# A new order of the seven products in a bidirectional encoder's Strassen-like projections

## The chip, the cores and the metric

The kernel runs on one core of a Trainium2 chip. The metric is device time in microseconds (us) of one execution; less is better. The core has engines that work side by side, each through a queue of its own: TensorE (PE in the profile, its weight loads PEld), VectorE (DVE), ScalarE (ACT), GpSimd (POOL) and SyncE (SP, which here only issues transfers). Matrix products land in PSUM, which the kernel divides into eight banks of 128 x 512 numbers.

## What is computed

One layer of an encoder over 1024 positions of width 1024, all in float32. A normalised input goes through one wide projection whose columns feed a convolution branch, a gated linear recurrence with eight heads in both directions, and two gates. The branches are merged, projected (w_out) and added to the input. A feed-forward part follows:

```python
h = _rmsnorm(x, attn_norm_w[layer])
y = _token_mixers(h, w_in[layer], ...)
x = x + jnp.einsum("bsd,de->bse", y, w_out[layer])
h2 = _rmsnorm(x, ffn_norm_w[layer])
gate, val = jnp.split(h2 @ ffn_w_up, 2, axis=-1)
x = x + (silu(dwconv3(gate)) * val) @ ffn_w_down
return _rmsnorm(x, final_norm_w)
```

The time goes into the matrix products: w_in (1024 x 8192 columns), ffn_w_up (1024 x 5632), and the smaller ones.

## The kernel before

**Numbers in two parts.** To keep float32's accuracy, each operand is split: ACT rounds it to a part "hi" (L121, a CAST in the profile), DVE subtracts that from the source for a part "lo" (L118). A product of a 128 x 128 block of weights with 128 x 512 activations is then three matmuls (`mm3`, lines L143, L144, L145): hi hi, hi lo, lo hi. The helper `split` does both steps; so the lines L121 and L118 stand for all splits, and only the names of the tiles tell them apart. Activations are kept as pages `hx` and `hy`, weights as `wp` (pool mp, 4 buffers) and `wq` (3 buffers).

**Pair jobs.** Two column blocks of 128 of a weight matrix are multiplied together by `pair_job` (L224), with seven products in place of eight, as Strassen and Winograd do it. The depth of 1024 is cut into two halves of four blocks (nk = 4), the positions into two halves of 512. Operands 1 to 7 on the side of the activations are sums and differences of the quarters, made once; operand 1, 2 and 3 are quarters themselves. On the side of the weights `prep` loads the rows of the first block (`wr`), the columns (`sw`) and the last quarter (`w4`), and lets POOL's accumulating transfers (L238) form sums: `sw` plus the second block, then `wr` plus half of `sw`, then one half of `wr` onto the other. Four splits lie between them: of `wr` for products 1 and 2, of `sw` for 7 and 5 (a `wq` pair of pages), of `wr` for 6 and 3, and of `w4` for 4 (the third `wq` page). `sw` and `w4` have one buffer each.

`run` multiplies: 12 matmuls a product, in the order 1, 2, 6, 7, 5, 4, 3 on three PSUM banks, `row` (of 3 banks "mm"), `b2` (of 2 "tr") and `col` (of 2 "sc"). A product may go on accumulating in a bank that has been copied out. ACT copies the banks after 1, 6 and 7 (L266, tiles `su`), and `evac(e, half, x0, x1, op)` takes a result out of the bank, e being the column block and half the half of the positions.

There are 39 pair jobs: 17 in the projection w_in (stage "in pairs", beside the convolution's 120 DVE operations on L645), 22 in the feed-forward part, where e = 0 is the gate and e = 1 the value. There, the gate's evacuation for half 1 starts the three-tap convolution, silu and the products with `rstd2` and the value (L1162 to L1180), ending in stores to `d_g`.

**Order of the work.** TensorE's instructions stand in the order of the program (`manual_schedule`). Those of the other engines are put in order before the run by the framework, which may draw an instruction forward as soon as its tiles and inputs are planned to be ready; each engine then works through its list in order and waits at whatever is not ready. `Stream` and `run_jobs` interleave jobs with other work: `run_jobs(..., 4)` prepares the next job's weights after four pieces (two products) of the current one.

**Memory.** Pools are stacked. `fw` (L1061) is opened after the heads' pool, before the output projection of the heads (`o_jobs`, L1083) and lives until the feed-forward part ends; `p4` above it holds `mg` (the merged branches, read by the w_out jobs), `x2` and `xq` and is released at L1136; `fu` (L1139) then takes p4's place. A tile in fu waits for the p4 tiles on whose memory it lies. After the feed-forward part `fd` takes the place of fw and fu; its first tiles are `xr`, which lie where `rstd2` was.

**Around the feed-forward part.** While w_out's jobs run, the normalised rows come out as `xq`; for each of the four k, operands 1, 2, 6 and 5 are made there (L1126 to L1135) into pages `hx`, and the rows are stored to `d_h2`. After two products of the first feed-forward job and the statistics for `rstd2` (L420 and L412 on TensorE), the "late" operands 7, 4 and 3 are made (L1209 to L1219): loads from `d_h2` through four `ft` pages, arithmetic on DVE, and a split into pages `hy`. Before that, `bm_loads` (L1002) loads and splits the operands of o_jobs through four `tm` pages. After the feed-forward part the down projection loads `d_g` through `ev` pages and splits it into `hx`; its first results are copied to `xr` (L1245).

Of the kernel before, what the change touches and what calls it, by code (L numbers as in the profile page):

```python
# [10 lines left out]
F32 = mybir.dt.float32  # L11
# [4 lines left out]
ALU = mybir.AluOpType  # L16
# [28 lines left out]
def tile_hybrid_encoder(  # L45
# [45 lines left out]
    def nm(s):  # L91
        uid[0] += 1
        return f"{s}_{uid[0]}"
# [3 lines left out]
    def bank(tag):  # L97
        return ps.tile([P, H], F32, tag=tag, name=nm(tag), bufs=BANKS[tag])
# [125 lines left out]
    def pair_job(src0, src1, nk, acts, wpool, pool, evac, su=4):  # L224

        def prep():
            def both(src, alt):
                hi, lo = split(w_page(2 * nk, alt), w_page(2 * nk, alt), src, V)
                return [(hi[:, :nk], lo[:, :nk]), (hi[:, nk:], lo[:, nk:])]

            def add(o, a):
                G.dma_start(o, a, accum_op=ALU.add)  # L238
# [48 lines left out]
    def combos(ops, k, b11, b12, b22, alloc):  # L287

        def sub(o, a, b):
            V.tensor_tensor(o, a, b, op=ALU.subtract)

        def parts(i, src):
            ops[i].append(split(alloc(), alloc(), src, V))

        t3 = page(mp, "tm", 4)
        sub(t3, b12, b22)
        parts(7, t3)
        sub(b22, t3, b11)  # L300
        parts(6, b22)
        sub(b12, b11, b12)
        parts(5, b12)
# [224 lines left out]
    for k in range(NK2):  # L528
        b21 = page(p1, "su", 4)
        nc.sync.dma_start(b21, d_h[k + NK2][0])  # L530
        for part in ht[6][k]:
            V.tensor_tensor(b21, b21, part.bitcast(F32), op=ALU.add)
        ht[4].append(split(hx(), hx(), b21, V))


# [46 lines left out]


    def store(dst, func=None):
        def evac(half, x0, x1=None, op=None):
            t = ev()
            if x1 is not None:
                V.tensor_tensor(t, x0, x1, op=op)
                x0 = t
            if func is not None:  # L590
                A.activation(t, x0, func)
            elif x1 is None:
                A.copy(t, x0)
            nc.sync.dma_start(dst[half], t)

        return evac
# [21 lines left out]
    def in_pair(n):  # L618
        (c0, e0), (c1, e1) = todo[2 * n], todo[2 * n + 1]
        evs = (e0, e1)  # L620
        return pair_job(
            in_cols(c0),
            in_cols(c1),
            NK2,
            lambda i: ht[i],
            p1,
            p1,
            lambda e, *quadrant: evs[e](*quadrant),
        )

    jobs = collections.deque(in_pair(n) for n in range(NPAIRS))
# [506 lines left out]

# [6 lines left out]

    def ffn_job(j):
        g = gp[j % 2]
        val = [None, None]

        def evac(e, half, x0, x1=None, op=None):  # L1150
            if e == 1:
                val[half] = page(fu, "ft", 4)
                V.tensor_tensor(val[half], x0, x1, op=op)  # L1153
                return
            gh = g[:, 1 + half * H : 1 + (half + 1) * H]
            if x1 is not None:
# [4 lines left out]
                return  # L1161
            for hf in range(2):  # L1162
                o = hf * H
                c = tmp()
# [14 lines left out]
                V.tensor_tensor(val[hf], val[hf], c, op=ALU.mult)  # L1179
                nc.sync.dma_start(d_g[j][hf], val[hf])  # L1180

        return pair_job(
            w_cols(ffn_w_up, 0, ND, j * P),
# [15 lines left out]
    rstd2 = [next(st) for st in stats]  # L1199

    def late_parts(i, src):
        h2[i].append(split(page(fu, "hy", 24, F32R), page(fu, "hy", 24, F32R), src, V))

    def late_load(kk, half):
        t = page(fu, "ft", 4)
# [1 line left out]
        return t  # L1207

    for k in range(NK2):  # L1209
        b12, b22 = late_load(k, 1), late_load(k + NK2, 1)  # L1210
        V.tensor_tensor(b12, b12, b22, op=ALU.subtract)
        late_parts(7, b12)
    for k in range(NK2):
        b21 = late_load(k + NK2, 0)
        for part in h2[6][k]:
            V.tensor_tensor(b21, b21, part.bitcast(F32), op=ALU.add)
# [155 lines left out]
```

## Time and profile before

| what | us |
|---|---|
| three timed runs | 1898.41, 1899.92 (median), 1903.82 |
| the profiled execution: its time / its span | 1905.6 / 1903.8 |
| in pairs and convolution | 140 to 485 |
| more of the projection, dense | 485 to 557 |
| the recurrence's heads beside the rest of the projection | 557 to 985 |
| o_jobs, from the first matmul to w_out's first | 999.7 to 1100 |
| w_out | 1100 to 1187 |
| first feed-forward job | 1186.8 to 1226.2 |
| the other 21 feed-forward jobs | 1226.2 to 1631.7 |
| down projection and output | 1631.7 to 1903.8 |

Times inside the execution count from the start of its span. In the stretches TensorE is busy for 334.0 of 345.1 us (in pairs), 397.6 of 428.0 (heads), 32.0 of 39.2 (first feed-forward job), 405.2 of 405.5 (the others) and 18.7 of 23.3 (1631.7 to 1655). A row of the timeline gives the start, the length, the engine, the line, the operation, the tiles as out<-in, and in square brackets the idle time of that engine just before and what ended it. A busy TensorE is not always at full pace: the granted clock tells how many of its pulses it was given.

### The profile page before, as it was taken

To read this page: it belongs to the slowest core of one execution; us is meant where nothing else is said; L and a number is where in the kernel's file an instruction comes from. 1 tells how busy PE (TensorE), PEld (TensorE's weight loads), DVE (VectorE), ACT (ScalarE), POOL (GpSimd) and SP (SyncE) were. 2 spreads that over 40 slices of the span, in tenths; PEclk is the share of its full clock that TensorE was granted. 3 is DMA by queue.
4 is the path that set the end of the run, shared out by engine and by line. 5 is a ranking of instruction groups with operands and counts; after the bars stand their busy time and mean duration, and the time that the engine had idled before them with its cause. 6 is when DMAs were issued, how large, how long until landed. Compare 5 with 4: busy or idle time off the path is not lost.

```text
span 1903.8 us, 23750 instructions
## 1 busy us (share of the span) xinstructions
PE 1799.7 (95%) x8543; PEld 1484.0 (78%) x8543; DVE 1270.2 (67%) x1860; ACT 799.2 (42%) x1488; POOL 210.9 (11%) x218
## 2 busy tenths in 40 slices
PE   6988999999999998999998999899999999999996
PEld 5767878887778887888786888588888888788885
DVE  3488999535469898999835555667676666534445
ACT  6433333234554554555443134544343344522124
POOL 3101111213100001000100000111111111000000
PEclk9999999999999999999998999899999999999998
DMA  7747788786563333342237665777676676733134
GB/s 256 219 119 169 179 188 199 185 182 148 190 192 89 113 108 96 111 122 82 75 95 216 197 200 183 185 153 154 147 151 143 143 156 128 221 93 96 54 89 162
DMA packets 323916, 285.09 MB, mean 150 GB/s; under 512 B 14926, under 2 KB 245078, under 8 KB 323798
## 3 DMA queue, kind: packets, MB, share of 16 engines
q1 hardware_dynamic: 272006, 242.67, 41.5%
q0 software_dynamic: 51792, 40.90, 15.2%
q8 instruction: 67, 1.10, 0.3%
q14 instruction: 51, 0.42, 0.1%
HBM read 191.24 MB, written 71.83 MB: 138 GB/s over the span
## 4 chain that ended last, share of the span: by engine, by line
PE 66%; DVE 13%; DMA 8%; ACT 6%; issue 3%; POOL 2%; SPq 0%; ACTq 0%; POOLq 0%; DVEq 0%
PE mm L143 16%; PE mm L144 16%; PE mm L145 16%; PE sc L144 3%; PE sc L145 3%; PE sc L143 3%; PE tr L143 2%; PE tr L144 2%; PE tr L145 2%; DVE wp L118 1%; DVE kG L730 1%; DVE DE L730 1%; PE sc L838 1%; DVE qF L730 1%; DMA wr<-wr 1%
## 5 line engine op out<-in xcount | busy, mean ns | idle before, releaser
L143 PE MATMUL mm<-hx,wp 128*128 128x512 f32 x1176 | 482.6, 410 | 24.6 <-ACT hx L121 8.6
L145 PE MATMUL mm<-hx,wp 128*128 128x512 f32 x1176 | 467.4, 397 | 3.9 <-DVE wp L118 3.9
L144 PE MATMUL mm<-hx,wp 128*128 128x512 f32 x1176 | 466.8, 397 | 2.9 <-POOL hx L118 1.9
L121 ACT CAST wp<-wr 128x1024 fp32r<-128x1024 f32 (+2 forms) x196 | 179.7, 917 | 323.0 <-PE mm L144 222.9
L143 PEld LDWEIGHTS mm<-hx,wp 128*128 128x128 f32 x1176 | 226.5, 193 | 73.7 <-ACT hx L121 9.5
L118 DVE TENSOR_TENSOR wp<-wr,wp 128x1024 fp32r<-128x1024 f32 (+2 forms) x196 | 206.9, 1056 | 102.9 <-ACT wp L121 97.4
L145 PEld LDWEIGHTS mm<-hx,wp 128*128 128x128 f32 x1176 | 225.5, 192 | 55.1 <-DVE wp L118 5.4
L144 PEld LDWEIGHTS mm<-hx,wp 128*128 128x128 f32 x1176 | 226.5, 193 | 48.4 <-POOL hx L118 3.6
L645 DVE SCALAR_TENSOR_TENSOR acc<-gl,v_b,acc 128x1024 f32<-128x1024 f32 x120 | 150.1, 1285 | 0.5
L143 PE MATMUL sc<-hy,wq 128*128 128x512 f32 x244 | 97.3, 399 | 3.1 <-ACT hy L121 3.0
L144 PE MATMUL sc<-hy,wq 128*128 128x512 f32 x244 | 96.7, 396 | 2.7 <-DVE hy L118 2.7
L145 PE MATMUL sc<-hy,wq 128*128 128x512 f32 x244 | 96.2, 394 | 0.0
L238 POOL DMA_DIRECT2D wr<-sw x39 | 34.9, 896 | 519.3 <-DVE wp L118 297.4
L1251 DVE TENSOR_TENSOR xr<-mm,xr 128x512 f32<-128x512 f32 x48 | 33.1, 690 | 82.0 <-PE mm L145 82.0
L838 PEld LDWEIGHTS sc<-qF,A 128*128 128x128 f32 x512 | 65.9, 193 | 19.0 <-issue 13.3
L838 PE MATMUL sc<-qF,A 128*128 128x128 f32 x512 | 69.1, 278 | 11.7 <-DVE qF L730 10.6
L121 ACT CAST wq<-sw 128x1024 fp32r<-128x1024 f32 x39 | 41.1, 1054 | 86.6 <-PE mm L144 66.4
L143 PE MATMUL mm<-hy,wp 128*128 128x512 f32 x156 | 63.2, 405 | 7.4 <-ACT wp L121 5.3
L266 ACT COPY su<-mm 128x512 f32<-128x512 f32 x78 | 45.5, 583 | 53.4 <-PE mm L145 53.4
L835 ACT COPY A<-kG 128x512 f32<-128x512 f32 x64 | 39.7, 620 | 66.3 <-DVE kG L730 37.8
L1169 DVE SCALAR_TENSOR_TENSOR tm<-gp,v_a,tm 128x512 f32<-128x512 f32 x88 | 65.6, 746 | 1.8 <-ACT tm L1165 0.9
L1153 DVE TENSOR_TENSOR ft<-su,mm 128x512 f32<-128x512 f32 x22 | 15.1, 687 | 71.6 <-issue 68.1
(281 smaller groups left out, 3548.6 us busy)
## 6 DMA issues: line engine op xcount, KB each, us to landing
wr<-in_w_in_dram SPq DMA_DIRECT2D x55, 512.0 KB, 6.5
sw<-in_ffn_w_up_dram SPq DMA_DIRECT2D x44, 256.0 KB, 3.5
sw<-in_ffn_w_up_dram POOLq DMA_DIRECT2D x22, 512.0 KB, 8.3
wr<-in_ffn_w_up_dram SPq DMA_DIRECT2D x22, 512.0 KB
d_g<-ft SPq DMA_DIRECT2D x44, 256.0 KB, 5.9
ev<-d_g SPq DMA_DIRECT2D x44, 256.0 KB, 3.2
wr<-sw POOLq DMA_DIRECT2D x39, 256.0 KB, 3.3
wr<-wr POOLq DMA_DIRECT2D x39, 256.0 KB, 3.8
```

What stands on the lines that cost most here:

```text
L118: eng.tensor_tensor(lo, src, hi.bitcast(F32), op=ALU.subtract)
L121: A.copy(hi, src)
L143: T.matmul(acc, whi[:, k, :], ahi, start=first, stop=False, skip_group_check=again)
L144: T.matmul(acc, whi[:, k, :], alo, start=False, stop=False, skip_group_check=again)
L145: T.matmul(acc, wlo[:, k, :], ahi, start=False, stop=last, skip_group_check=again)
L238: G.dma_start(o, a, accum_op=ALU.add)
L266: A.copy(t, acc)
L645: V.scalar_tensor_tensor(acc, g[:, k : k + S], tap(k), acc, op0=ALU.mult, op1=ALU.add)
L730: V.tensor_tensor(o, a, b, op=op)
L835: A.copy(A_t.rearrange("p (b x e) -> p b x e", x=2, e=h), pairs(kG, h))
L838: T.matmul(b[:, c * P : (c + 1) * P].rearrange("p (b x e) -> p b x e", x=2, e=h), A_t[:, c * P : (c + 1) * P], view(qF, c * P, [[2 * h, P ...
L1169: V.scalar_tensor_tensor(c, g[:, o + k : o + k + H], vec("fdw", k * NF + j), c, op0=ALU.mult, op1=ALU.add,)
```

## The change

The seven products run in the order 1, 2, 6, 5, 7, 3, 4. Products 1, 6, 7 and 4 accumulate in `row`; 2 has `b2`; 5 and 3 accumulate in `b5`, a second bank of the kind "mm"; no "sc" bank is used. The copies to SBUF come after 1, 6 and 5. Operands 7 and 4 are made with the opposite sign, so `row` ends as minus the quarter (1, 0): that evacuation takes the bank alone and turns its sign, in ACT's `scale` or in the product with the gate. Evacuation (1, 1) is minus the bank minus the copy, by a scalar_tensor_tensor operation (`sub_both`). In the feed-forward part operand 7 is made beside 1, 2, 6 and 5 in w_out's stage, into eight pages `h7` of pool fw; the late operands are then 3 and, after it, 4. The pages `wq` and `w4` of `pair_job` come from the pool `fu` and not from `fw` in the feed-forward part (in the in pairs both are `p1`). The value is multiplied with the gate by `join`, which for half 0 reads the bank of product 4 directly.

```diff
-            a22 = wpool.tile([P, nk, P], F32, tag="w4", name=nm("w4"), bufs=1)
+            a22 = pool.tile([P, nk, P], F32, tag="w4", name=nm("w4"), bufs=1)
...
-            w[7], w[5] = both(col, wpool)
+            w[7], w[5] = both(col, pool)
...
-            one = w_page(2 * nk, wpool)
+            one = w_page(2 * nk, pool)
...
-            row, b2, col = bank("mm"), bank("tr"), bank("sc")
+            row, b2 = bank("mm"), bank("tr")
             yield from product(1, row)
             p1 = copy(row)
             yield from product(2, b2)
             evac(0, 0, b2, p1, ALU.add)
             yield from product(6, row, False)
             u2 = copy(row)
-            yield from product(7, col)
-            p7 = copy(col)
-            yield from product(5, row, False)
-            evac(1, 1, p7, row, ALU.subtract)
-            yield from product(4, col, False)
-            evac(1, 0, col, u2, ALU.subtract)
-            yield from product(3, row, False)
-            evac(0, 1, row)
+            b5 = bank("mm")
+            yield from product(5, b5)
+            r5 = copy(b5)
+            yield from product(7, row, False)
+            evac(1, 1, row, r5, None)
+            yield from product(3, b5, False)
+            evac(0, 1, b5, u2, ALU.add)
+            yield from product(4, row, False)
+            evac(1, 0, row, None, None)
...
+    def sub_both(o, a, b):
+        V.scalar_tensor_tensor(o, a, -1.0, b, op0=ALU.mult, op1=ALU.subtract)
+
+    def less_parts(o, hl):
+        sub_both(o, o, hl[0].bitcast(F32))
+        V.tensor_tensor(o, o, hl[1].bitcast(F32), op=ALU.subtract)
...
     h2_pages = {i: [(hx(), hx()) for _ in range(NK2)] for i in (1, 2, 6, 5)}
+    h2_pages[7] = [[page(fw, "h7", 2 * NK2, F32R) for _ in range(2)] for _ in range(NK2)]
...
-        t5, t6 = tmp(), tmp()
+        t7, t6, t5 = tmp(), tmp(), tmp()
         parts(1, k, b11)
+        V.tensor_tensor(t7, b22, b12, op=ALU.subtract)
+        parts(2, k, b21)
+        sub_both(t6, t7, b11)
+        parts(6, k, t6)
         V.tensor_tensor(t5, b11, b12, op=ALU.subtract)
-        parts(2, k, b21)
-        V.scalar_tensor_tensor(t6, t5, -1.0, b22, op0=ALU.mult, op1=ALU.subtract)
-        parts(6, k, t6)
         parts(5, k, t5)
+        parts(7, k, t7)
...
+        def join(hf, x0, sign):
+            V.scalar_tensor_tensor(val[hf], x0, sign, gate[hf], op0=ALU.mult, op1=ALU.mult)
+            nc.sync.dma_start(d_g[j][hf], val[hf])
...
     for k in range(NK2):
-        b12, b22 = late_load(k, 1), late_load(k + NK2, 1)
-        V.tensor_tensor(b12, b12, b22, op=ALU.subtract)
-        late_parts(7, b12)
+        late_parts(3, late_load(k + NK2, 1))
     for k in range(NK2):
         b21 = late_load(k + NK2, 0)
-        for part in h2[6][k]:
-            V.tensor_tensor(b21, b21, part.bitcast(F32), op=ALU.add)
+        less_parts(b21, h2[6][k])
         late_parts(4, b21)
-    for k in range(NK2):
-        late_parts(3, late_load(k + NK2, 1))
```

The same sign changes are made for the projection w_in, in `combos` and where operand 4 is made (L528), with as many operations as before.

More of the change, by code (lines that the diff above doesn't have):

```diff
@@ L295, in parts @@
             ops[i].append(split(alloc(), alloc(), src, V))
[L297 to L300, printed above, removed]
+        t7 = page(mp, "tm", 4)
+        sub(t7, b22, b12)
+        parts(7, t7)
+        sub_both(b22, t7, b11)
         parts(6, b22)
@@ L530, in tile_hybrid_encoder @@
         nc.sync.dma_start(b21, d_h[k + NK2][0])
-        for part in ht[6][k]:
-            V.tensor_tensor(b21, b21, part.bitcast(F32), op=ALU.add)
+        less_parts(b21, ht[6][k])
         ht[4].append(split(hx(), hx(), b21, V))
@@ L584, in store, with evac @@
     def store(dst, func=None):
-        def evac(half, x0, x1=None, op=None):
+        def evac(half, x0, x1=None, op=None, sign=1.0):
             t = ev()
             if x1 is not None:
-                V.tensor_tensor(t, x0, x1, op=op)
+                if op is None:
+                    sub_both(t, x0, x1)
+                else:
+                    V.tensor_tensor(t, x0, x1, op=op)
                 x0 = t
             if func is not None:
-                A.activation(t, x0, func)
+                A.activation(t, x0, func, scale=sign)
             elif x1 is None:
-                A.copy(t, x0)
+                A.activation(t, x0, AF.Copy, scale=sign)
             nc.sync.dma_start(dst[half], t)
@@ L627, in in_pair @@
             p1,
-            lambda e, *quadrant: evs[e](*quadrant),
+            lambda e, half, x0, x1, op: evs[e](half, x0, x1, op, -1.0 if x1 is None else 1.0),
         )
@@ L1147, in ffn_job @@
         g = gp[j % 2]
[L1148 removed]
+        val, gate = [None, None], [None, None]
+        def join(hf, x0, sign):
+            V.scalar_tensor_tensor(val[hf], x0, sign, gate[hf], op0=ALU.mult, op1=ALU.mult)
+            nc.sync.dma_start(d_g[j][hf], val[hf])
         def evac(e, half, x0, x1=None, op=None):
@@ L1152, in evac @@
                 val[half] = page(fu, "ft", 4)
-                V.tensor_tensor(val[half], x0, x1, op=op)
+                if x1 is None:
+                    join(half, x0, -1.0)
+                elif op is None:
+                    sub_both(val[half], x0, x1)
+                else:
+                    V.tensor_tensor(val[half], x0, x1, op=op)
                 return
@@ L1163, in evac @@
                 o = hf * H
-                c = tmp()
+                c = gate[hf] = tmp()
                 A.activation(
@@ L1178, in evac @@
                 V.tensor_tensor(c, c, rstd2[hf], op=ALU.mult)
-                V.tensor_tensor(val[hf], val[hf], c, op=ALU.mult)
-                nc.sync.dma_start(d_g[j][hf], val[hf])
+            join(1, val[1], 1.0)
         return pair_job(
@@ L1201, in late_parts @@
     def late_parts(i, src):
-        h2[i].append(split(page(fu, "hy", 24, F32R), page(fu, "hy", 24, F32R), src, V))
+        h2[i].append(split(page(fu, "hy", 16, F32R), page(fu, "hy", 16, F32R), src, V))
     def late_load(kk, half):
```

1 line of the change is left out of this document (removed).

## The prediction

> **What bounds the kernel now.** I read the page's busy table and clock row first, then TensorE's waits over the whole span, then the chain, the timeline and the busy time by stretch around each long wait. The page (engine, busy us, share, instructions; then the granted clock in tenths, 40 slices):
>
> ```profile
> PE 1799.7 (95%) x8543; PEld 1484.0 (78%) x8543; DVE 1270.2 (67%) x1860; ACT 799.2 (42%) x1488; POOL 210.9 (11%) x218
> ...
> PEclk9999999999999999999998999899999999999998
> ```
>
> TensorE (PE) is the bound, and the change keeps its number of matmuls: each pair job has 7 products of 12 matmuls before and after. A steady pair of the first projection takes 19.04 us (product 2 starts at 343.42 and at 362.46), which is 84 x 0.2267. So only PE's 104 us of idle time, and its stretches at a lower clock, can be won. The pair jobs have few waits once they run: feed-forward's follow each other every 19.25 us. Three places stand out, all beside pair jobs. (start us, us, engine, line, operation, [idle before <-releaser]):
>
> ```profile
> 1002.34 0.39 PE L145 MATMUL mm<-hx,wp 128*128 128x512 f32 x1
> 1011.00 0.79 PE L143 MATMUL mm<-hx,wp 128*128 128x512 f32 x1 [8.27 <-ACT hx L121]
> 1012.79 0.80 PE L144 MATMUL mm<-hx,wp 128*128 128x512 f32 x1 [1.00 <-DVE hx L118]
> ...
> 1200.05 0.49 PE L143 MATMUL sc<-hy,wq 128*128 128x512 f32 x1 [0.49 <-ACT hy L121]
> 1201.74 0.51 PE L144 MATMUL sc<-hy,wq 128*128 128x512 f32 x1 [1.20 <-DVE hy L118]
> 1203.00 0.73 PE L143 MATMUL sc<-hy,wq 128*128 128x512 f32 x1 [0.52 <-ACT hy L121]
> ...
> 1644.65 0.79 PE L143 MATMUL mm<-hx,wp 128*128 128x512 f32 x1 [4.61 <-ACT xr L1245]
> ```
>
> Place A is the start of the output projection of the heads (o_jobs), B the first feed-forward job, C the start of the down projection. Why A waits stands on ScalarE (ACT):
>
> ```profile
> 998.92 0.63 ACT L121 CAST hx<-tm 128x512 fp32r<-128x512 f32 x1 [0.25 <-DMA tm<-d_bm]
> 1007.43 1.04 ACT L121 CAST wq<-sw 128x1024 fp32r<-128x1024 f32 x1 [7.88 <-DMA sw<-in_ffn_w_up_dram]
> 1010.34 1.65 ACT L121 CAST hx<-tm 128x512 fp32r<-128x512 f32 x3
> ```
>
> A cast of the first feed-forward job's weights (wq<-sw), needed only 190 us later, stands in ACT's queue ahead of the casts that o_jobs wait for, and waits 7.88 us for its accumulating DMA (10.75 us in the chain, from 996.66). The price also holds a slow phase (stretch; length; PE, PEld, DVE, ACT, POOL busy; granted clock; DMA share; GB/s):
>
> ```profile
> 1011.00:1018.60 7.60, 6.60 (x15) 4.84 (x16) 5.58 (x9) 3.82 (x7) 0.00 (x0) 0.50 0.84 268
> 1203.00:1213.40 10.40, 7.87 (x15) 4.34 (x16) 6.61 (x11) 2.34 (x4) 0.87 (x1) 0.51 0.81 224
> ```
>
> At a clock of 0.50 matmuls start every 0.427 us in place of 0.227.
>
> **The change, part by part.** All sums go from the profiled execution: 1905.6 us, span 1903.8. The three timed runs have a median of 1899.92, so a difference is taken from that.
>
> *A, feed-forward's wq and w4 pages move from pool fw to fu.* fu takes the memory of p4, whose mg pages the out projection reads until 1186.8, so no wq cast can be queued at 1007 any more. Before, A cost 8.27 + 1.00 of waiting and 18 matmuls x 0.20 = 3.6 of slow clock: 12.9. What is late next is the load itself: tm<-d_bm was issued at 999.42 and such loads land after 2.6 to 3.8 us (median 3.6), so at 1003.0; cast 0.62 and subtraction 0.69 follow, while PE is through with k=3 at 1002.6. That leaves some 1.8 us of waits. The second half's seven loads go round four tm pages (some 5 us a round: 3.6 + 0.62 + 0.69) and are needed from 1012.4; up to 2 us may be late there. Without a slow phase the gain is 11.1, with a whole one 7.5. I take 8; bounds 0 (another early cast takes the place) and 11.
>
> The row at 1203 shows that waits of 0.49, 1.20 and 0.52 within 4 us were enough for the clock to fall, which is why I take the lower part. The Trainium skill, "TensorE: Matmul & The Clock Gate", section "Why this matters for your kernels", would have only an idle gap of about 3 us or more cost the clock; by it the rest of A stays fast and A gives 11, the total 1876. The trace speaks against it.
>
> *B, operand 7 made in the out projection's stage, late operands 3 and 4 in the order of need.* Before, from product 1 (1186.83) to the next job's product 1 (1226.18) take 39.35 us. 19.04 are matmuls and 4.0 the statistics' own (L420 and L412), so 16.3 are lost: 6.9 in waits, the rest in slow clock and restarts. Product 7 came fourth and waited for eight loads and four subtractions through four ft pages; the loads landed after 4.4 to 7.4 us (median 5.9) since DMA is at 0.97 from 1187 to 1198.6. The change takes away eight loads of 256 KB on SP's queue, four subtractions and four splits there (8 x 0.69 DVE, 4 x 0.62 ACT). In the out projection's stage it adds the same four subtractions and splits: from 1100 to 1187 DVE is busy 45.4 of 87 us, ACT 36.2, and PE has no gap, so three of four are free; if that cover went, each would cost PE up to 2 us. The fourth falls to 1188 to 1194, and its product starts at 1202.
>
> Then products 1, 2, 6, 5, 7 run without late loads, until some 1204.7 (1186.8 + 4.0 + 5 x 2.72, and 0.3 for restarts). Operand 3's four loads (issued about 1190, landing by 1197) need only a split each. Operand 4's loads follow when ft pages come free, about 1199.5, landing about 1204.5; then DVE has four times sub_both 0.69, subtraction 0.69, split 0.69, with evac(1,1) 0.69 and a weight split 1.22 between: 10.2 us, so operand 4 is whole at 1214.7 and product 4 ends near 1215.5, or 1217 with a part at the low clock. Gain 9. Bounds: 16 (no wait left) and 2 (DVE, busy 26.5 of the 39.2 us, remains the limit).
>
> Job 0's wq split (ACT 1.05, DVE 1.22) and w4 split (0.62, 0.69) and w4's load on SP now come here too. They need mg pages read last by 1183.5; product 5 starts at 1199. Fifteen microseconds cover them. What waits behind: sw is held until that split, where its release at 1181.97 let job 1's load go. If it goes at 1190, it lands 6.0 later, and the add of 8.3 and two row adds (3.3 and 3.8, with issues 9) end about 1213, against product 6 of job 1 at about 1221: covered. Held until 1197, it is just in time.
>
> *C, the product order's end.* 3 is now sixth and 4 last. The last job's gate then leaves its bank 2.72 us earlier, and so do rstd2's last reads (L1178, 1638.73), whose memory xr takes. Copies of xr came at 1644.02, behind two hx casts waiting for ev loads, themselves behind d_g stores on SP. Cost before: 4.6 + 12 x 0.20 = 7. I take 4 off; bounds 7 and -1 (casts queued otherwise).
>
> *Second bank, order, signs.* Copies and evacuations were each covered by a product of 2.72 us on another bank, and are still: 6 waits for p1's copy behind 2, 7 for u2 behind 5, 3 for r5 behind 7, 4 for evac(1,1) behind 3. Three mm banks suffice: b5 takes the bank of the last job's row, 8 us after its end. No bank wait is removed, none added: 0. If DVE is late as at 259.61 it costs 1.9 there, as before. Scaled ACT copies cost what L591 does (591 ns beside 578 for L593). Feed-forward keeps 13 DVE operations a job.
>
> sub_both has a constant scalar. Its nearest row is L1133, 128x512 between SBUF pages: 684 ns, as the plain subtraction L1131 (683): 0. Of the Trainium skill, "Vector Engine (DVE) Microarchitecture Reference", section "Points that are easy to get wrong", says that this operation runs at half throughput with two non-bf16 SBUF sources; by it the four on B's path would add 2.7 and the total be 1882. The row of 684 ns decides against it.
>
> *Steady feed-forward.* POOL's row add waits for the stores of d_g:
>
> ```profile
> 1315.23 0.89 POOL L238 DMA_DIRECT2D wr<-sw x1 [8.27 <-DMA d_g<-ft]
> 1323.34 1.05 ACT L121 CAST wp<-wr 128x1024 fp32r<-128x1024 f32 x1 [2.40 <-DMA wr<-wr]
> ```
>
> The stores move some 3 us earlier and wp's pages 3/6 come free 2.72 earlier, so this chain gains slack; jobs that took 19.55 and 19.76 may give back 0.8. Matmuls start every 0.230 in parts of these jobs and every 0.2264 in the first projection, which no row explains: bounds -4.7 and +3.7 if one took the other's pace; I take 0.
>
> Sum: -8 - 9 - 4 = -21: 1884.6 for the profiled execution, **1879** against the median.
>
> **Rivals.** (1) A's wait finds another owner: ACT's queue holds other casts whose data come late, as the two at C. For it: the order is set by a planner that thought sw's data ready. Against: no other cast near 1000 belongs to a later stage. -13: 1887.
> (2) B stays DVE- and DMA-bound, or w4 and sw come late: B gives 2. For: DMA at 0.97, DVE's 10 us for operand 4. -14: 1886.
> (3) Both: the gaps only move, -2 to -5 at most: 1897.
> (4) Slower: feed-forward's sw page becomes the period. Its round is load 6.0, add 8.3, row add 3.6: 17.9 of 19.25. If with the moved stores the adds take 10.75 (as at 996.66) and 4.3 (as at 1488), it is 21.05, or 1.8 more in each of 22 jobs: +39 - 21: 1918. It decides once the adds grow by 1.4 us. Against: the stores leave earlier, DMA's share is 0.70 there.
>
> **How the numbers follow.** Forecast 0.52, (1) 0.17, (2) 0.13, (3) 0.08, (4) 0.10. Low end: A 11, B 16, C 7 together are 1866; I put 1865. High end 1898 takes in (1) to (3) and leaves (4) out. 0.3%, about what a measurement of this kernel can tell from no change, is 5.7 us: faster 0.82 (forecast, 1, 2), same 0.08 (3), slower 0.10 (4).
>
> **What would show it.** A right: no wq<-sw cast on ACT near 1007, and a PE wait under 2.5 us there. B right: the first feed-forward job under 32 us, its last waits in product 4 and on DVE. C right: the wait on xr under 2 us. Wrong if another ACT cast waits on a DMA ahead of o_jobs' casts, if product 5 or 7 waits in job 0, or if later jobs' period passes 19.5.

## The result, and the profile after

| | us, median | ratio to before, 95% interval |
|---|---|---|
| before | 1900.7 | |
| after | 1916.7 | 1.0078 [1.0061, 1.0094] |

The kernel became slower by 0.8%, where 1879 us were forecast, with a range of 1865 to 1898. The profiled execution after has a span of 1914.4 us (before 1903.8). Cut at the first matmul of product 2 in certain pair jobs, the two spans compare so (us):

| stretch | before | after | difference | forecast |
|---|---|---|---|---|
| start to pair job 1 | 139.9 | 138.5 | -1.4 | 0 |
| pair jobs 1 to 17 (in pairs) | 326.2 | 334.7 | **+8.4** | 0 |
| to feed-forward's first job (holds A) | 725.1 | 716.1 | -9.0 | -8 |
| first feed-forward job (B) | 38.1 | 38.9 | **+0.8** | -9 |
| the next 20 feed-forward jobs | 385.9 | 400.0 | **+14.2** | 0 |
| from there to TensorE's last row (C) | 275.8 | 273.5 | -2.3 | -4 |

Stretches of unchanged code differ between single profiles too: in the runs below the pair jobs in the old order take 323.4 to 327.9 us with one `sw` page, and the stretch that holds the recurrence and A takes 713.4 to 725.1 us. A term of that stretch is therefore read from its waits.

The page before, its chain by engine:

```profile
PE 66%; DVE 13%; DMA 8%; ACT 6%; issue 3%; POOL 2%; SPq 0%; ACTq 0%; POOLq 0%; DVEq 0%
```

The page after, its busy table and chain (by engine, then by line):

```profile
PE 1796.4 (94%) x8543; PEld 1478.3 (77%) x8543; DVE 1268.8 (66%) x1860; ACT 797.6 (42%) x1488; POOL 213.9 (11%) x218
...
PE 44%; DMA 23%; DVE 18%; ACT 7%; issue 5%; POOL 2%; SPq 1%; ACTq 0%; POOLq 0%; DVEq 0%
PE mm L143 13%; PE mm L144 13%; PE mm L145 13%; DMA wr<-wr 5%; DMA wr<-sw 4%; DMA sw<-in_ffn_w_up_dram 4%; DVE wp L118 2%; DVE acc L658 2%; DMA sw<-in_w_in_dram 2%; DMA d_g<-ft 2%; ACT wp L121 2%; DVE kG L743 1%; DVE DE L743 1%; DVE qF L743 1%; PE sc L851 1%
```

The work is the same: each engine has as many instructions as before, and PE's busy time moves by 3 us. The chain of work that ended last shows the difference. It ran for 66% through PE and now runs for 44%, and what came in is the preparation of pair weights: the row additions (`wr<-wr`, `wr<-sw`), the accumulation on `sw`, the casts and subtractions of `wp`. TensorE's waits after (total us, times, longest):

```profile
PE mm L143 <- ACT su L267: 12.3, 16, 2.5
PE mm L143 <- DVE ft L291: 12.2, 1, 12.2
...
PE mm L143 <- DVE ev L291: 8.6, 5, 3.0
```

Before had none of the three at that size. The first stands for 9.0 us in the 20 later feed-forward jobs, 7.0 of it at product 6 (its longest, 2.5, is in a pair job); the second is product 4 of the first feed-forward job, the third product 4 of pair jobs. Each leads back to the cast of the next job's weights 6 and 3, which waits for the second row addition.

**Steady feed-forward.** One late job after, by SP, POOL, ACT and PE (each row: start, length, engine, line, operation, idle before and its releaser):

```profile
1401.16 0.38 SPq L244 DMA_DIRECT2D sw<-in_ffn_w_up_dram  x1
...
1407.08 1.58 POOL L239 DMA_DIRECT2D sw<-in_ffn_w_up_dram  x1 [5.58 <-DMA sw<-in_ffn_w_up_dram]
1407.41 0.37 SPq L130 DMA_DIRECT2D wr<-in_ffn_w_up_dram  x1
...
1409.34 0.37 SPq L247 DMA_DIRECT2D w<-in_ffn_w_up_dram  x1
...
1418.28 0.89 POOL L239 DMA_DIRECT2D wr<-sw  x1 [9.62 <-DMA sw<-in_ffn_w_up_dram]
...
1421.87 0.86 POOL L239 DMA_DIRECT2D wr<-wr  x1 [2.70 <-DMA wr<-sw]
...
1427.32 1.05 ACT L121 CAST wp<-wr 128x1024 fp32r<-128x1024 f32 x1 [7.96 <-DMA wr<-wr]
...
1430.86 0.57 ACT L267 COPY su<-mm 128x512 f32<-128x512 f32 x1
...
1431.48 0.50 PE L143 MATMUL mm<-hx,wp 128*128 128x512 f32 x1 [2.06 <-ACT su L267]
```

Read it from below. Product 6 waits for the copy of product 1's bank, the copy stands in ACT's list behind the cast of weights 6 and 3, and that cast waits 7.96 us for the second row addition. The addition is late because from the accumulation on `sw` to the first addition it took 11.2 us (1407.08 to 1418.28). Over the 19 later jobs that have one it takes 8.2 to 11.9 us, median 9.7; before 7.8 to 10.2, median 8.8. In its flight now lie the loads of `wr` (512 KB) and `w4` (256 KB): in the median they are issued together with the accumulation and 1.9 us behind it, where before `w4`'s left 3.0 us ahead and `wr`'s 1.3 us behind. `wr`'s page comes free with the earlier cast of 6 and 3, and `w4`'s only behind product 4, now the last. That these loads lengthen the accumulation is not shown: in e2 below they stand at the same places, and it takes 8.1 to 11.6 us, median 8.9.

Two things meet in the wait. Weights 6 and 3 share pages that are read until product 3 ends. Product 3 was seventh and is sixth, so those pages come free about 13.75 us after product 2's start and no longer at 16.5; the framework therefore put the next job's cast ahead of `w4`'s cast (the gate's activation and p1's copy stood behind it before, too). But its data, whose second addition is issued at about 11.2 of the same count in the quiet jobs and is 3.8 us on the way (the page's median), arrive at about 15: before with 1.5 us to spare, now 1.2 us after ACT could have begun. Whoever stands behind it in ACT's and DVE's lists waits too, and when the accumulation is slow, as here, that reaches product 6.

**The first feed-forward job.** ACT, DVE, DVE, PE, after:

```profile
1217.01 1.04 ACT L121 CAST wp<-wr 128x1024 fp32r<-128x1024 f32 x1 [7.15 <-DMA wr<-wr]
1218.09 1.22 DVE L118 TENSOR_TENSOR wp<-wr,wp 128x1024 fp32r<-128x1024 f32 x1 [5.94 <-ACT wp L121]
...
1219.83 0.68 DVE L291 SCALAR_TENSOR_TENSOR ft<-mm,su 128x512 f32<-128x512 f32 x1
...
1220.67 0.77 PE L143 MATMUL mm<-hy,wq 128*128 128x512 f32 x1 [12.15 <-DVE ft L291]
```

Product 4 needs the bank that evac(1,1) reads (1219.83). This stands on DVE behind the subtraction for job 1's weights 6 and 3, which waits for their cast, which waits for the row addition. The load of job 1's `sw` left at 1193.9 (before at 1182.0), so the addition was late; the 12.15 us ate the whole of B.

**The pair jobs.** ACT, DVE, DVE, DVE, PE, after:

```profile
203.69 1.05 ACT L121 CAST wp<-wr 128x1024 fp32r<-128x1024 f32 x1 [5.80 <-DMA wr<-wr]
204.77 1.23 DVE L118 TENSOR_TENSOR wp<-wr,wp 128x1024 fp32r<-128x1024 f32 x1 [2.83 <-ACT wp L121]
...
217.66 4.86 DVE L658 SCALAR_TENSOR_TENSOR acc<-gl,v_b,acc 128x1024 f32<-128x1024 f32 x4
222.45 0.68 DVE L291 SCALAR_TENSOR_TENSOR ev<-mm,su 128x512 f32<-128x512 f32 x1
...
223.19 0.50 PE L143 MATMUL mm<-hx,wq 128*128 128x512 f32 x1 [3.05 <-DVE ev L291]
```

The same two rows before, without a wait:

```profile
203.06 1.03 ACT L121 CAST wp<-wr 128x1024 fp32r<-128x1024 f32 x1
...
204.75 1.22 DVE L118 TENSOR_TENSOR wp<-wr,wp 128x1024 fp32r<-128x1024 f32 x1
```

Here it is DVE that loses time: 2.83 us at the subtraction, with the convolution's operations behind it; evac(1,1) then stands late behind four of these, and product 4 waits. DVE has little room to catch up here: before it is busy for 219.5 of the 280 us from 160 to 440 and waits for the weights' casts for another 21.

**A and C.** The first row is o_jobs' start (before 8.27 and 1.00), the second the down projection's (before 4.61), both on PE after:

```profile
1010.38 0.50 PE L143 MATMUL mm<-hx,wp 128*128 128x512 f32 x1 [2.27 <-ACT hx L121]
...
1657.35 0.50 PE L143 MATMUL mm<-hx,wp 128*128 128x512 f32 x1 [2.06 <-ACT xr L1264]
```

### The profile page after: what moved, and what is told of

Read it like the earlier page. It is cut to its first block, busy times and chain, and to the rows that moved or that the text cites. A ratio compares the mean times of both kernels' runs of the same rounds, so it can differ in the third digit from the quotient of the medians.

```text
span 1914.4 us, 23701 instructions
## 1 busy us (share of the span) xinstructions
PE 1796.4 (94%) x8543; PEld 1478.3 (77%) x8543; DVE 1268.8 (66%) x1860; ACT 797.6 (42%) x1488; POOL 213.9 (11%) x218
## 4 chain that ended last, share of the span: by engine, by line
PE 44%; DMA 23%; DVE 18%; ACT 7%; issue 5%; POOL 2%; SPq 1%; ACTq 0%; POOLq 0%; DVEq 0%
PE mm L143 13%; PE mm L144 13%; PE mm L145 13%; DMA wr<-wr 5%; DMA wr<-sw 4%; DMA sw<-in_ffn_w_up_dram 4%; DVE wp L118 2%; DVE acc L658 2%; DMA sw<-in_w_in_dram 2%; DMA d_g<-ft 2%; ACT wp L121 2%; DVE kG L743 1%; DVE DE L743 1%; DVE qF L743 1%; PE sc L851 1%
## 5 line engine op out<-in xcount | busy, mean ns | idle before, releaser
L267 ACT COPY su<-mm 128x512 f32<-128x512 f32 x117 | 67.4, 581 | 101.3 <-PE mm L145 100.6
L143 PE MATMUL mm<-hy,wq 128*128 128x512 f32 x224 | 89.4, 399 | 12.2 <-DVE ft L291 12.2
L144 PE MATMUL mm<-hy,wq 128*128 128x512 f32 x224 | 88.2, 394 | 0.0
L145 PE MATMUL mm<-hy,wq 128*128 128x512 f32 x224 | 87.9, 393 | 0.0
L851 PE MATMUL sc<-qF,A 128*128 128x128 f32 x512 | 68.3, 276 | 11.1 <-DVE qF L743 10.2
L143 PE MATMUL mm<-hx,wq 128*128 128x512 f32 x156 | 62.8, 402 | 8.7 <-DVE ev L291 8.6
L848 ACT COPY A<-kG 128x512 f32<-128x512 f32 x64 | 39.7, 620 | 66.3 <-DVE kG L743 37.8
L291 DVE SCALAR_TENSOR_TENSOR ft<-mm,su 128x512 f32<-128x512 f32 x22 | 15.2, 691 | 76.4 <-issue 71.3
```

What stands on the lines that cost most here:

```text
L143: T.matmul(acc, whi[:, k, :], ahi, start=first, stop=False, skip_group_check=again)
L144: T.matmul(acc, whi[:, k, :], alo, start=False, stop=False, skip_group_check=again)
L145: T.matmul(acc, wlo[:, k, :], ahi, start=False, stop=last, skip_group_check=again)
L848: A.copy(A_t.rearrange("p (b x e) -> p b x e", x=2, e=h), pairs(kG, h))
L851: T.matmul(b[:, c * P : (c + 1) * P].rearrange("p (b x e) -> p b x e", x=2, e=h), A_t[:, c * P : (c + 1) * P], view(qF, c * P, [[2 * h, P ...
```

## The experiments

All were timed beside the kernel before. "Pairs": pair jobs 1 to 17; "DVE": DVE's waits there, from 150 to 430 us, at the weights' subtractions for their casts; "first": the first feed-forward job; "next 20" as above; all in us of the profiled execution.

| run | median | ratio, 95% interval | pairs | DVE | first | next 20 |
|---|---|---|---|---|---|---|
| before | | | 326.2 | 21.3 | 38.1 | 385.9 |
| after | 1916.7 | 1.0078 [1.0061, 1.0094] | 334.7 | 30.2 | 38.9 | 400.0 |
| e1, pools alone | 1891.2 | 0.9966 [0.9947, 0.9985] | 326.3 | 14.2 | 36.6 | 384.7 |
| e2, order alone | 1913.3 | 1.0082 [1.0057, 1.0106] | 334.8 | 29.5 | 41.2 | 386.7 |
| e3, pools and early 7, old order | 1883.6 | 0.9918 [0.9890, 0.9945] | 327.9 | 23.0 | 26.2 | 387.9 |
| e4, after + second sw, feed-forward | 1895.5 | 0.9985 [0.9968, 1.0001] | 334.5 | 28.6 | 37.6 | 385.1 |
| e5, after + second w4, feed-forward | 1904.4 | 1.0030 [1.0013, 1.0047] | 338.0 | 32.0 | 37.8 | 391.8 |
| e6, after + second sw, both parts | 1886.9 | 0.9923 [0.9903, 0.9942] | 318.7 | 5.4 | 37.8 | 385.1 |
| e7, e3 + second sw, feed-forward | 1891.9 | 0.9950 [0.9933, 0.9967] | 323.4 | 22.6 | 27.5 | 387.1 |
| e8, before + second sw, feed-forward | 1902.5 | 1.0004 [0.9986, 1.0021] | 323.9 | 20.6 | 39.7 | 385.1 |
| e9, after, 6 and 3 held to the end | 1910.1 | 1.0064 [1.0039, 1.0089] | 342.6 | 33.3 | 33.3 | 388.6 |
| e10, e3 + second sw, both parts | 1883.4 | 0.9917 [0.9898, 0.9937] | 319.0 | 9.1 | 28.0 | 388.1 |
| e11, after + second w4, both parts | 1906.1 | 1.0025 [1.0004, 1.0046] | 331.7 | 31.4 | 35.6 | 393.6 |
| e12, e9 + second w4, both parts | 1909.3 | 1.0054 [1.0032, 1.0076] | 342.7 | 34.5 | 32.8 | 387.6 |
| e13, e9 + own pages for w4 | 1917.8 | 1.0107 [1.0083, 1.0131] | 340.8 | 31.7 | 37.1 | 393.2 |
| e14, after + own pages for w4 | 1907.4 | 1.0045 [1.0023, 1.0066] | 338.5 | 29.9 | 37.9 | 393.0 |

**e1 to e4: which part costs, and is it the single sw page?** Theory: the cost comes from the order of the products. Rival: the pages in the later pool hold `sw` longer, and its round never catches up.

e1 is the kernel before with the change's first three lines:

```diff
-            a22 = wpool.tile([P, nk, P], F32, tag="w4", name=nm("w4"), bufs=1)
+            a22 = pool.tile([P, nk, P], F32, tag="w4", name=nm("w4"), bufs=1)
-            w[7], w[5] = both(col, wpool)
+            w[7], w[5] = both(col, pool)
-            one = w_page(2 * nk, wpool)
+            one = w_page(2 * nk, pool)
```

> The kernel before, with only the wq and w4 pages of the feed-forward part moved from pool fw to fu. Theory P (the move holds job 0's sw page longer, and the chain of sw's load, add and row adds then never catches up): place A gains about 9 us, the first feed-forward job and the 20 after it lose up to 15, so 1892 to 1907, with product 2 of the first and last feed-forward job more than 395 us apart less the first job. Theory O (the new order of the products is what costs): A's gain alone, 1890 to 1893, and the 20 steady feed-forward jobs take 386 us as before.

The pools alone are a gain: 7.9 us below the kernel before in the same comparison, with a wait of 2.70 at o_jobs' start. Nineteen of the later jobs take 19.22 us. So the move of the pages costs nothing in the old order.

e2 is the changed kernel with these three lines taken back, operand 7 late again, and the late operands in the order 7, 3, 4:

```diff
-    h2_pages[7] = [[page(fw, "h7", 2 * NK2, F32R) for _ in range(2)] for _ in range(NK2)]
...
+    for k in range(NK2):
+        b12, b22 = late_load(k, 1), late_load(k + NK2, 1)
+        V.tensor_tensor(b12, b22, b12, op=ALU.subtract)
+        late_parts(7, b12)
```

> The changed kernel, with wq and w4 back in pool fw and operand 7 made late again (with the new sign; late operands in the order 7, 3, 4). Theory O: the in pairs stage loses its 8.4 us and the 20 steady feed-forward jobs their 14 us here too, and A gains nothing, so about 1920. Theory P: the in pairs stage loses 8.4, the steady feed-forward jobs take 386 us as before, so about 1907.

The order alone ends as far above the kernel before as the whole change, but without its gains: +8.6 in the pair jobs, and +3.1 in the first feed-forward job, where product 4 waits 9.4 us; there evac(1,1) stands on DVE behind the work for the late operands, not behind an idle wait. In the later jobs it costs only 0.8, as the rival had it, though two of them (21.0 and 20.2 us) show the wait for p1's copy. So the loss of the pair jobs needs the new order alone, and the 14 us need it together with the pools or the early 7; which of the two was not separated. A late start of `sw` is not the link: in the second feed-forward job of the changed kernel the first addition comes 5.8 us after product 2, as before.

e3 is the kernel before with the pools of e1 and operand 7 made early into `h7`, in the old order and with the old signs.

> The kernel before in its old order of products and signs, with operand 7 of the feed-forward part made early into pool fw, the pages wq and w4 moved to fu, and the late operands 4 and 3. Theory O: A gains 9, the first feed-forward job some 5, nothing is lost in the in pairs stage or the steady jobs: 1885 to 1892. Theory P: the steady jobs lose up to 14 as in the changed kernel: 1895 to 1906.

It beats both kernels. Its first feed-forward job takes 26.2 us in place of 38.1: behind the statistics no product in it waits for as long as 0.3 us, and PE's next wait stands in the second job:

```profile
1216.48 0.50 PE L143 MATMUL mm<-hx,wp 128*128 128x512 f32 x1 [1.49 <-ACT su L266]
```

e4 lets feed-forward's jobs take `sw` from two pools in turn, which makes two pages:

```diff
-            col = wpool.tile([P, 2 * nk, P], F32, tag="sw", name=nm("sw"), bufs=1)
+            col = (spool or wpool).tile([P, 2 * nk, P], F32, tag="sw", name=nm("sw"), bufs=1)
...
             su=3,
+            spool=fu if j % 2 else fw,
```

> The changed kernel with a second page for sw in the feed-forward part (even jobs use one in fw, odd jobs one in fu). If the round of the single sw page (load, add, row add, load) is the period that the steady jobs wait for, under theory P as under theory O, the 20 jobs take 386 us in place of 400 and the total is about 1902. If the jobs wait because ACT's queue has the cast for products 6 and 3 ahead of product 1's copy, whatever sw does, they stay at 400 and the total at 1917.

The later jobs are back at 19.25 us each. POOL and ACT in one of them:

```profile
1422.01 0.89 POOL L239 DMA_DIRECT2D wr<-sw  x1 [5.62 <-DMA d_g<-ft]
...
1425.64 0.86 POOL L239 DMA_DIRECT2D wr<-wr  x1 [2.73 <-DMA wr<-sw]
...
1430.06 1.05 ACT L121 CAST wp<-wr 128x1024 fp32r<-128x1024 f32 x1 [1.72 <-PE mm L144]
```

The row addition waits for the stores of d_g and no longer for `sw`, it starts 5.8 us after product 2 (9.3 to 11.2 in the jobs of the changed kernel ahead of a late one), and the cast waits for PE to leave its page, not for a DMA. This shows that the 14 us come through the single `sw` page. The pair jobs, which keep one page here, stay at 334.5.

**e5 to e8: the same in the pair jobs, and controls.** e5 gives feed-forward a second page for w4's raw load (`bufs=w4`, 2 there).

> The changed kernel with two pages instead of one for w4's raw load in the feed-forward jobs, nothing else: that load may then leave before product 4 of the job before has freed the page, so it no longer falls into the flight of the accumulating load on sw. Theory A (the two loads that now run beside the accumulation lengthen sw's round): the 20 later feed-forward jobs fall from 400.0 us to 390 or less and the kernel to about 1907. Theory B (the single sw page's own round is the period, and what runs beside it adds little): they stay at 396 to 402 and the kernel at 1914 to 1919.

It gives back 8.2 of the 14.2 us, between the two expectations and nearer to the first. But the second page did not move the load. It still follows `wr`'s on SP, behind the accumulation in each of these jobs (1.5 us in the median, 1.9 after):

```profile
1268.44 1.58 POOL L239 DMA_DIRECT2D sw<-in_ffn_w_up_dram  x1 [5.23 <-DMA sw<-in_ffn_w_up_dram]
1268.59 0.37 SPq L130 DMA_DIRECT2D wr<-in_ffn_w_up_dram  x1
1270.52 0.37 SPq L247 DMA_DIRECT2D w<-in_ffn_w_up_dram  x1
```

So e5 doesn't test the loads in the accumulation's flight. The accumulation and its wait average 9.3 us here (9.9 after, 9.0 before); why the page shortens them stays open.

e6 is e4 with two `sw` pages in the pair jobs as well:

```diff
+            sw=2,
```

> The changed kernel with a second page for sw in both places: two in the conv pairs' pool, and the feed-forward jobs alternate between two pools as in the run before. Theory A (product 3 is now sixth, so the cast and the subtraction of weights 6 and 3 are put a product earlier into the lists of ScalarE and VectorE, ahead of the moment when the second row addition has landed, and VectorE stands there with evac(1,1) behind it): the row additions come about 4 us earlier, the waits of TensorE on VectorE at product 4 go, the 16 pair jobs fall from 334.6 us to 326 to 328, the kernel to 1883 to 1890 us, 0.992 of the kernel before. Theory B (VectorE is simply too full in this order, or the new banks hold it): the pair jobs stay at 333 to 336 and the kernel at 1893 to 1897, as with the feed-forward page alone.

Theory A held, and by more than expected: 318.7 us, less than in any profile with one page. DVE's waits at the weights' subtractions from 150 to 430 us (total, times, longest), in the kernel before:

```profile
DVE wp L118 <- ACT wp L121: 21.3, 7, 6.7
```

In the changed kernel:

```profile
DVE wp L118 <- ACT wp L121: 30.2, 13, 7.2
```

In e6:

```profile
DVE wp L118 <- ACT wp L121: 5.4, 7, 2.4
```

With the second row addition 3.5 us earlier (median, counted from product 2), DVE stands for 5.4 us where it stood for 30.2. Over all runs the stage's length goes with that wait from group to group: 14 to 23 us in the old order (323 to 328), 28 to 35 in the new (332 to 343), under 10 with two pages (319 in both orders, e6 and e10). Within the old order it does not sort the runs.

e7 is e3 with e4's lines, e8 the kernel before with them.

> The kernel before with its order of products and signs, operand 7 made early, the w4 and wq pages of the feed-forward jobs in the later pool, and a second sw page in the feed-forward jobs. If sw's round still costs anything in the old order, the excess of the second and fourth feed-forward job (1.8 and 0.6 us in the run without the second page) goes: about 1881 us. If it doesn't, it stays at 1883.6. Product 3 is last here, so the weights 6 and 3 have a product more time: the pair jobs should stay at 326 to 328 us.

> The kernel before with a second sw page in the feed-forward jobs and nothing else: a control. If the second page helps only where sw is held late (the changed kernel), this is within 2 us of the kernel before, 1899 to 1901, with 385 to 386 us for the 20 later feed-forward jobs. If it is a gain of its own, it falls by 5 or more in the first feed-forward job.

e8 changes nothing, so in the feed-forward part the page helps only where `sw` is late. e7's profiled execution (span 1883.2) is shorter than e3's (1886.9), but its median is 8 us above e3's; the expected 1881 did not come, and why its other runs were longer is open. Of the excess of the second and fourth feed-forward job the fourth's went (19.28), the second's stayed (20.8).

**e9 to e14: later casts, earlier loads.** e9 keeps one `sw` page and holds the pages of 6 and 3 to the end of the job: the `True` leaves out product 3's last matmul, which is issued behind product 4, and evac(0,1) moves there with it:

```diff
...
-            yield from product(3, b5, False)
-            evac(0, 1, b5, u2, ALU.add)
+            yield from product(3, b5, False, True)
             yield from product(4, row, False)
+            T.matmul(b5, w[3][1][:, nk - 1, :], acts(3)[nk - 1][0], start=False, stop=True, skip_group_check=True)
+            evac(0, 1, b5, u2, ALU.add)
             evac(1, 0, row, None, None)
```

> The changed kernel, all its work kept, with the last of product 3's twelve matmuls moved behind product 4, so that the pages of weights 6 and 3 come free at the end of the job as before, and their cast and subtraction stand about 2.5 us later in the lists; evac(0,1) and evac(1,0) follow it. One sw page, as in the changed kernel. Theory A (the cost is the place of 6 and 3 in the lists of ScalarE and VectorE): the pair jobs fall from 334.6 to 325 to 329 us, the 20 later feed-forward jobs from 400 to 386 to 391, the 12.2 us wait in the first feed-forward job to under 4; the kernel to 1878 to 1894. Theory B (the late sw round alone makes the loss, wherever the cast stands): the pair jobs stay at 333 to 338, the feed-forward jobs at 396 to 402, the kernel at 1912 or more.

The first expectation held in feed-forward (388.6, and the wait at product 4 fell from 12.15 to 2.87) and failed in the pair jobs, 342.6, and in the total. ACT waits there even longer for the row additions (from 150 to 430 us; 45.4 us after, 22.4 before):

```profile
ACT wp L121 <- DMA wr<-wr: 65.2, 11, 8.2
```

From the accumulation's issue to the row addition it takes 10.1 us on average over these jobs (9.7 after, 9.0 before), and the second addition starts 14.9 us after product 2 in the median (13.8 after): the cast is held back, but its data come later as well. Why was not tested.

> The kernel before with its order of products and signs, operand 7 made early, the w4 and wq pages of the feed-forward jobs in the later pool, and a second sw page in the pair jobs as well as in the feed-forward jobs. If the earlier row additions help the old order as they helped the new one (318.7 us for the pair jobs), its pair jobs fall from 323 to 328 to about 319 and it is the fastest yet, 1876 to 1884. If the old order has no wait there that they can remove, it stays at 1884 to 1892, as without the pages of the pair jobs.

e10, the old order with e3's parts and both second pages, has the pair jobs at 319.0 as expected, so the single page cost the old order some 7 us there, too. It and e3 are the fastest, 0.9917 and 0.9918, which can't be told apart: the 9 us by which its pair jobs are shorter in the profile do not show in its median, and why is open.

e11 has w4's second page in both parts, e12 that and e9's hold. e13 and e14 give w4's split weights two pages of their own (with the hold, and without), and `wq` then has two buffers in place of three:

```diff
-            one = w_page(2 * nk, pool)
+            one = pool.tile([P, 2 * nk, P], F32R, tag="wf", name=nm("wf"), bufs=2)
```

> The changed kernel with two pages for w4's raw load in the pair jobs as well as in the feed-forward jobs. Only w4's 256 KB move out of the accumulation's flight; the cast of 6 and 3 stays where it is in the lists, and wr's 512 KB still follow sw. Theory A (the two loads beside the accumulation delay the row additions in the pair jobs as they did in the feed-forward part): the pair jobs fall from 334.6 us to 327 to 331, the kernel to about 1898 to 1904. Theory B (there it is VectorE's list, in which evac(1,1) stands behind the subtraction of 6 and 3): they stay at 333 to 338 and the kernel at 1902 to 1909, as with the feed-forward page alone.

> Both at once: the last matmul of product 3 behind product 4, so that 6 and 3 are cast at the end of the job, and two pages for w4's raw load in the pair jobs and the feed-forward jobs. Theory A (place in the lists and the loads in the accumulation's flight are the whole of the loss): the pair jobs come back to 324 to 329 us, the 20 later feed-forward jobs to 385 to 388, and the kernel to 1878 to 1890. Theory B (the pair jobs' loss has another root, VectorE's load in this order): the pair jobs stay above 333, and the kernel at 1892 to 1905.

> The changed kernel with the last matmul of product 3 behind product 4, and with two weight pages of their own for w4 (both in the pair jobs and in the feed-forward jobs), so that w4's cast and subtraction no longer wait for product 4 of the job before and stand ahead of those of 6 and 3, as in the kernel before, and its raw load leaves early. Theory A (in the pair jobs it is the order of the weights' preparation in the lists, 6 and 3 last, that the kernel before had and the change lost): the pair jobs come back to 324 to 330 us, the kernel to 1880 to 1895. Theory B (something else in the new order, as evac(0,1) on VectorE now following product 3, or banks): they stay at 333 or more, the kernel above 1895.

> The changed kernel with the two weight pages of its own for w4 and nothing else: 6 and 3 are cast as soon as product 3, now sixth, has ended. Theory A1 (6 and 3 cast ahead of the landing of the second row addition is the cost in the pair jobs): they stay at 330 to 336 us here. Theory A2 (the cost is w4's late load and late preparation): they come back to 324 to 329. The feed-forward jobs, where w4's load alone gave back 8 of 14 us, should be at 390 to 394.

e11's pair jobs (331.7) lie between the theories; 3 us are inside the scatter of that stage. e12, e13 and e14 stay at 342.7, 340.8 and 338.5 there. (e14's later feed-forward jobs, 393.0, came as expected.) But they do not settle what the place of the casts costs, for none of them brings back the old place: in every profile of the new order, with the hold and without, the cast of 6 and 3 directly follows that of `sw`'s weights among the casts of weights, and `w4`'s comes behind it. ACT in e13:

```profile
218.54 1.06 ACT L121 CAST wq<-sw 128x1024 fp32r<-128x1024 f32 x1 [1.90 <-PE mm L144]
...
226.03 1.05 ACT L121 CAST wp<-wr 128x1024 fp32r<-128x1024 f32 x1 [1.31 <-DMA wr<-wr]
229.63 0.62 ACT L121 CAST wf<-w 128x512 fp32r<-128x512 f32 x1 [2.56 <-PE mm L145]
```

In the old order `w4`'s stands between the two. Nor did `w4`'s load leave the accumulation's flight in the pair jobs of e11 and e12. Of all runs in the new order only the one with earlier row additions, e6, brings these jobs back. There, as the lists suggest, the round is closed through DVE: a late addition stops DVE, the late DVE delays the subtraction of `sw`'s weights, this delays the next load of `sw`. Shown is that a second `sw` page ends the loss, and that with it both orders take the same; which of the round's links the new order lengthens first in these jobs stays open.

## Why the prediction was wrong

- **A (-8): right.** The waits fell from 9.27 to 2.72 us, the longest to 2.27, under the 2.5 named, the granted clock of the 7.6 us behind them rose from 0.50 to 0.78, and e1, the pools alone, gained 7.9. That the stretch fell by just 9.0 is in part luck: in e1 it falls by 2.3.
- **B (-9): the reasoning on operands is borne out in the old order, the cover of the weights was not.** With the old order (e3) early 7 and the pools bring the first job to 26.2, 11.9 us less; in the new order, with the wait at product 4 down to 2.87 (e9), it still takes 33.3. The step that failed is "Held until 1197, it is just in time". Its chain was sized well, 23.0 us from `sw`'s load at 1193.9 to the landing of the second addition where the sum had 23.3; but only product 6 of job 1 was looked at as a consumer. The addition's cast and subtraction stand in ACT's and DVE's lists ahead of job 0's evac(1,1), so product 4 of job 0 paid, 12.15 us.
- **C (-4): right in kind.** The wait on xr fell from 4.61 to 2.06 (named: under 2), the stretch by 2.3. Over all runs the stretch takes 273.9 to 276.6 us in the old order and 270.7 to 273.5 in the new.
- **"Second bank, order, signs ... 0": the largest error in the pair jobs, +8.4.** The bank side was worked out rightly: with two `sw` pages the new and the old order take 318.7 and 319.0 us, so order, bank and signs cost nothing of themselves, and `sub_both` takes medians of 684 to 692 ns in all its forms. But a product's place also sets when its weight pages come free, and with one `sw` page the two orders take 334.7 and 326.2.
- **"wp's pages 3/6 come free 2.72 earlier, so this chain gains slack" (steady feed-forward, 0): the sign was wrong, +14.2.** A page that comes free earlier lets the framework draw its cast forward in an in-order list; the data behind it did not come earlier. The row in the prediction's own fence, a cast at 1323.34 that waited 2.40 us for `wr<-wr`, had no slack to give.
- **Rival (4), slower, was the right mechanism** with 0.10: `sw`'s round outlasted the job where the accumulation grew, to 11.2 us where it named 10.75. It cost 14 and not 39, since only some jobs were late (seven of 20.5 to 23.3 us), and it named moved stores as the reason; what lengthens the accumulation is open. It had not seen the pair jobs, where the same round runs through a DVE with little room. That its total, 1918, lies next to the measured 1916.7 is chance: the loss is made of 14.2, of 8.4 in the pair jobs and of a B that was lost.
- Rival (2) named "w4 and sw come late" for B, and `sw` did come late, but through the lists of ACT and DVE and at product 4; B gave -0.8 where it had 2. Rivals (1) and (3) have no place in the result, since A came whole. The sign that later jobs' period would pass 19.5 showed in eight of the 20 jobs (before, in two).

## What to carry to other kernels

When a step moves earlier, its buffers come free earlier, and whatever is drawn forward into them will stand in an in-order list: compare the new start with the landing of its data, and name everything behind it in that list. A transfer chain through a single page (here load, accumulation, two additions, cast) is a loop with a period; work out its slack against the job's period. Test a suspected loop by a second page: here it took the whole loss away, while the edits beside it gave back a part in one stage and little or nothing in the other. And look in the trace whether an edit moved what it was meant to move: e5, e11 and e13 did not.

## What the runs showed of the hardware

- The clock after single waits. From 150 to 430 us in all profiles, matmuls behind a single wait of 1 to 1.75 us keep a pitch of 0.229 to 0.234 us; behind single waits of 3.1 us or more the next eight average 0.37 to 0.43; between 1.86 and 3.05 both occur (2.95 us: 0.229; 2.31 us: 0.426). The Trainium skill, "TensorE: Matmul & The Clock Gate", section "Why this matters for your kernels", has gaps of about 3 us or more cost the clock. For single waits the runs agree from there on, better than the prediction granted; shorter ones are not safe.
- A 512 KB accumulation took 7.2 to 7.7 us to the next step in the first pair job, where no other weight load was issued within 2.5 us of it (13 profiles). Where a 512 KB load was issued within 0.6 us of it and a 256 KB load 1.3 to 2.6 us behind, it took 8.1 to 12.4 us (63 cases with one `sw` page in that part), without a rule that the runs show.
- The scalar_tensor_tensor operation with two float32 SBUF sources (`ft<-ft,hx`) takes 690 ns for 128 x 512 (687 to 693), like a plain subtraction (681 to 684).
